# A two-layer transformer and a second block on one core: layer norm behind the experts on VectorE alone, a shift added in TensorE's sums

## The chip, the core and the metric

The kernel runs on one core of a Trainium2 chip. A core has TensorE (matmuls and transposes, results in PSUM), VectorE (DVE), ScalarE (ACT), GpSimd (POOL) and SyncE (SP, which here issues most of the DMAs). Each works off its own queue in order. The metric is the device time of one execution in microseconds, the median of several runs.

## The reference, cut to what matters

A first block (two layers of mixer, layer norm, experts, layer norm) feeds a second block (two layers of three mixers behind a modulated RMS norm). All is f32, 1024 tokens by 1024 features. The places that the change touches are the second layer norm of each layer of the first block, and the input of the second block's first layer:

```python
def layer_norm(x, g, b):
    mu = mean(x); var = mean((x - mu) ** 2)
    return (x - mu) * rsqrt(var + LN_EPS) * g + b

# first block, layers i = 0 and 1
h = layer_norm(ALPHA * h + mix, ln_g[i, 0], ln_b[i, 0])
ffn = hier_moe(h, ...)
h = layer_norm(ALPHA * h + ffn, ln_g[i, 1], ln_b[i, 1])

# second block, layers l = 0 and 1
shift, scale, gate = split(c_act @ ada_w[l] + ada_b[l], 3)
h = rms_norm(x, norm_w[l]) * (1 + scale) + shift
proj = h @ w_in[l]
...
x = x + gate * (mixed @ w_out[l])
```

## The kernel before

The 1024 tokens lie in eight tiles of 128 tokens by 1024 features. Behind each layer of experts a stretch of the program takes these tiles one after the other from the experts' results in DRAM (`yd`) to the matrices that the next gemms read.

`Moe.combine` (L895) loads a tile's two expert rows through SP (L898), adds them on VectorE (L899) and calls `norm_stats`, which takes the statistics (L503, twice 512 columns, then L505 and L507), gets rs as a power on GpSimd (L137, in `Ctx.rsqrt`) and the product -mean x rs on VectorE (L510). `norm_apply` (L514) then scales and moves the tile on ScalarE (L518), multiplies it by the gain on VectorE (L519) and adds the bias on GpSimd (L520).

In the first stretch (L2023 to L2030, behind the first layer's experts) the tile is turned by TensorE at once (`transpose_split`, L98) and split by ScalarE (L80) and VectorE (L81) into two parts for the gemms of `Pooling.run`. Two parts of gemms on the first four tiles run while the last tiles come; from then on the gemms need all eight.

In the second stretch (`feed`, L2070, behind the second layer's experts) the normed tile is stored to `x1d` by SP (L2078). `take_input` squares and sums it on ScalarE (L1201), gets a second power on GpSimd (L1202, L137), multiplies on VectorE by rs and by 1 + scale times the norm's weight (L1209), and adds the shift on GpSimd (L1210). `turn_input` turns the tile in eight transposes of 128 by 128 into PSUM (L1219), ScalarE copies the rounded part out (L80) and VectorE takes the rest (L81). The steps of a tile are spread over the calls of a loop: in step n come the statistics of tile n, the norm of n - 1, the input of n - 2, the turning of n - 3. `first_tiles` (L1264) calls `feed` four times and then has four times 48 matmuls of 256 columns, one group for each two tiles; they write two accumulators, and VectorE's L1278 reads the first of them afterwards. The same `take_input` and `turn_input` serve the second block's second layer, called from `Second.layer`.

`self.mod` holds two rows spread over all 128 partitions (L1184): scale in `mod[:, 0]`, shift in `mod[:, 1]`. `g.one_row` is one row of 128 ones.

The code gives each engine its instructions in program order with waits, but the framework's planner reorders them: it runs the program with its own durations and gives each engine, whenever it is free, the earliest instruction that is ready. What it has put in a queue stays in that order on the chip.

Of the kernel before, what the change touches and what calls it, by code (L numbers as in the profile page):

```python
# [10 lines left out]
F32 = mybir.dt.float32  # L11
# [3 lines left out]
AF = mybir.ActivationFunctionType  # L15
ALU = mybir.AluOpType
# [5 lines left out]
P = 128  # L22
NT = S // P
# [474 lines left out]
def norm_stats(g, pool, z, eps=1e-5):  # L498

    nc = g.nc  # L500
    st = pool.tile([P, 2, 6], F32, tag="ln_st", name=g.name("st"))
    for c in range(2):
        nc.vector.bn_stats(st[:, c], z[:, c * 512:c * 512 + 512])  # L503
    mv = pool.tile([P, 2], F32, tag="ln_mv", name=g.name("mv"))
    nc.vector.bn_aggr(mv, st)  # L505
    v = pool.tile([P, 1], F32, tag="ln_v", name=g.name("v"))
    nc.vector.tensor_scalar(v, mv[:, 1:2], eps, None, op0=ALU.add)  # L507
    rs = g.rsqrt(pool, v, [P, 1])
    sh = pool.tile([P, 1], F32, tag="ln_sh", name=g.name("sh"))
    nc.vector.scalar_tensor_tensor(sh, mv[:, 0:1], -1.0, rs, op0=ALU.mult, op1=ALU.mult)  # L510
    return rs, sh


def norm_apply(g, z, stats, gb):  # L514

    nc = g.nc
    rs, sh = stats
    nc.scalar.activation(z, z, AF.Identity, scale=rs, bias=sh)  # L518
    nc.vector.tensor_mul(z, z, gb[:, 0])  # L519
    nc.gpsimd.tensor_tensor(z, z, gb[:, 1], op=ALU.add)  # L520


def load_gb(g, pool, tag, layer, n):
    gb = pool.tile([P, 2, D], F32, tag=tag, name=g.name("gb"))
    for j, a in enumerate((g.a["ln_g"], g.a["ln_b"])):
        g.nc.sync.dma_start(gb[:, j], a[layer, n:n + 1].broadcast_to([P, D]))
    return gb


class Moe:  # L530
# [4 lines left out]
    @staticmethod  # L535
    def rows(w, kb):
        return w[kb * 512:kb * 512 + 512].rearrange("(a p j) c -> p a (j c)", p=P, j=2), 512
# [357 lines left out]
    def combine(self, t, y, z, pool):  # L895

        g, nc = self.g, self.g.nc
        self.yload = nc.sync.dma_start(y, self.yd.rearrange("(k t p) d -> t p k d", k=2, p=P)[t])  # L898
        nc.vector.tensor_add(z, y[:, 0], y[:, 1])  # L899
        return norm_stats(g, pool, z)  # L900
# [266 lines left out]
class Second:  # L1167
# [34 lines left out]
        nc.vector.tensor_scalar(ss, ss, 1.0 / D, 1e-6, op0=ALU.mult, op1=ALU.add)  # L1202
        return g.rsqrt(pool, ss, [P, 1])

    def take_input(self, t, x, pool, hn=None):
        g, nc = self.g, self.g.nc
        hn = pool.tile([P, D], F32, tag="hn", name=g.name("hn")) if hn is None else hn
        rs = self.rms(x, hn, pool)
        nc.vector.scalar_tensor_tensor(hn, x, rs, self.mod[:, 0], op0=ALU.mult, op1=ALU.mult)  # L1209
        nc.gpsimd.tensor_tensor(hn, hn, self.mod[:, 1], op=ALU.add)  # L1210
        return hn

    def turn_input(self, t, hn, tp=None):
        g, nc = self.g, self.g.nc
        if tp is None:
            tp = self.PS.tile([P, S], F32, tag="tp", name=g.name("tp"))
        tp = tp.rearrange("p (k t) -> p k t", t=P)
        for k in range(KD):
            nc.tensor.transpose(tp[:, k], hn[:, k * P:k * P + P], g.ident)  # L1219
        g.split(tp, *(x[:, :, t % 4 * P:t % 4 * P + P] for x in self.x2[t // 4]))  # L1220


# [719 lines left out]
def program(tc, a, out):  # L1942
    nc = tc.nc
    g = Ctx(tc, a)
# [6 lines left out]
    x1d, x2d = dram("x1d", (S, D)), dram("x2d", (S, D))  # L1951
# [3 lines left out]
    rows = lambda ap, t: ap[t * P:t * P + P]  # L1955

    with pool_of("const") as cp, ExitStack() as r2:
# [40 lines left out]
        with near("rt", 1) as rt:  # L1998
            moe = Moe(g, 0, wp, rt, h, hd, yd)
            gb = load_gb(g, R, "r7", 0, 0)  # L2000
# [14 lines left out]
            gbs = []  # L2015
# [3 lines left out]
        with near("pm", 2) as pool, near("pmps", 4, space=PSUM) as ps:  # L2019
            with near("hT", 1, side="right") as tp:  # L2020
                x2 = [[tp.tile([P, KD, 512], F32R, name=f"pool_{half}{part}") for part in range(2)] for half in range(2)]
                with near("cb0ps", 2, space=PSUM) as tps:
                    h = single(pairs())  # L2023
                    for t in range(NT):
                        if t % 2 == 0:
                            y = H.tile([P, 2, 2, D], F32, tag="wcut", name=g.name("y"))
                        z = h[t]
                        norm_apply(g, z, moe.combine(t, y[:, t % 2], z, pool), gbs[0])
                        sl = slice(t % 4 * P, t % 4 * P + P)
                        g.transpose_split(even_blocks(z.rearrange("p (k d) -> p k d", d=P)), *(x[:, :, sl] for x in x2[t // 4]), tps)  # L2030
                W = []

                def out_piece(pool, tag):
                    W.append(g.split_w(wp.load(proj_piece(a["pool_w_out"][0], len(W))), pool, tag))
                pooling.run(x2, pool, ps, moe.yload.ins, lambda: out_piece(*cut))
            w1 = ExitStack()
            wx = w1.enter_context(near("wo", 2, side="right"))
            out_piece(wx, "w")
            out_piece(wx, "w")
            out_piece(*cut)  # L2040
        wp.use(slots)
        with near("rt1", 1) as rt:
            moe1 = Moe(g, 1, wp, rt, h, hd1, yd1)
            gb = load_gb(g, R, "r7", 1, 0)
# [5 lines left out]
            gbs, L = [], Second(g, H, R, md, zd, mixd, rd, qrd, rrd, x2d)  # L2050
# [14 lines left out]
        with ExitStack() as cb:  # L2065
            pool = cb.enter_context(L.pool("cb1", 3))
            L.start_layer()
            xs, stats, hn = [], [], []

            def feed(q):  # L2070
                for n in range(2 * q + 3 if q else 0, 2 * q + 5):
                    if n < NT:
                        y = R.tile([P, 2, D], F32, tag=f"r{(0, 1, 2, 3, 7)[n % 5]}", name=g.name("y"))
                        xs.append(y[:, 0])
                        stats.append(moe1.combine(n, y, xs[n], pool))
                    if 0 <= n - 1 < NT:
                        norm_apply(g, xs[n - 1], stats[n - 1], gbs[0])
                        nc.sync.dma_start(rows(x1d, n - 1), xs[n - 1])  # L2078
                    if 0 <= n - 2 < NT:
                        hn.append(L.take_input(n - 2, xs[n - 2], pool))  # L2080
                    if n >= 3:
                        L.turn_input(n - 3, hn[n - 3], L.ps("B"))
                if q == 3:
                    cb.close()

            L.layer(feed, x1d, None)
# [31 lines left out]
```

## Time and profile before

| what | us |
|---|---|
| median of three runs | 3568.6 (3566.94 to 3578.99) |
| the profiled execution | 3576.12 |
| its span, first to last instruction | 3574.3 |
| TensorE busy in it | 3308.5 (93%) |
| VectorE busy | 2424.9 (68%) |
| ScalarE busy | 1818.0 (51%) |
| GpSimd busy | 817.6 (23%) |

The profile is one execution. PE is TensorE, PEld its weight loads, DVE VectorE, ACT ScalarE, POOL GpSimd; SPq is SyncE's queue. In a row of the order of time stand the start, the duration, engine, line and operation, what is written and read, how many instructions are merged, and, in brackets, how long the engine was idle before it and what ended that. A row of waits gives the total, how often and the longest. PEclk is TensorE's granted clock as a share of 2.4 GHz; it has two levels, 1.00 and 0.50, and values between are mixtures.

### The profile page before, as it was taken

To read this page: it belongs to the slowest core of one execution; us is meant where nothing else is said; L and a number is where in the kernel's file an instruction comes from. 1 tells how busy PE (TensorE), PEld (TensorE's weight loads), DVE (VectorE), ACT (ScalarE), POOL (GpSimd) and SP (SyncE) were. 2 spreads that over 40 slices of the span, in tenths; PEclk is the share of its full clock that TensorE was granted. 3 is DMA by queue.
4 is the path that set the end of the run, shared out by engine and by line. 5 is a ranking of instruction groups with operands and counts; after the bars stand their busy time and mean duration, and the time that the engine had idled before them with its cause. 6 is when DMAs were issued, how large, how long until landed. Compare 5 with 4: busy or idle time off the path is not lost. (4 is left out here: it accounts for less than half of the span.)

```text
span 3574.3 us, 44065 instructions
## 1 busy us (share of the span) xinstructions
PE 3308.5 (93%) x16808; PEld 2738.9 (77%) x16808; DVE 2424.9 (68%) x2850; ACT 1818.0 (51%) x2505; POOL 817.6 (23%) x583
## 2 busy tenths in 40 slices
PE   8889899899999969989999994899989899998988
PEld 7777787788888858778888883787777788776876
DVE  5564887799999976569999997533366444424653
ACT  3113674388888843337888883122467311243751
POOL 0000441123333322112333324422002113400120
PEclk9999999899999989989999996999999999998999
DMA  6564633499999950259999995210322632122244
GB/s 225 179 209 143 162 85 130 172 359 389 376 379 378 353 214 24 96 177 368 385 390 383 378 348 197 60 30 19 111 77 87 190 111 43 24 80 100 66 136 153
DMA packets 289357, 695.78 MB, mean 195 GB/s; under 512 B 43898, under 2 KB 140956, under 8 KB 272692
## 3 DMA queue, kind: packets, MB, share of 16 engines
q1 hardware_dynamic: 268404, 650.91, 52.4%
q0 software_dynamic: 18432, 33.60, 2.5%
q10 hardware_dynamic: 2304, 8.39, 0.6%
q8 instruction: 135, 2.21, 0.3%
q14 instruction: 82, 0.67, 0.1%
HBM read 625.59 MB, written 98.66 MB: 203 GB/s over the span
## 5 line engine op out<-in xcount | busy, mean ns | idle before, releaser
L81 DVE TENSOR_TENSOR wcut<-wraw,wcut 128x2048 fp32r<-128x2048 f32 (+1 forms) x401 | 902.6, 2268 | 74.9 <-ACT wcut L80 74.8
L80 ACT ACTIVATE wcut<-wraw 128x2048 fp32r<-128x2048 f32 (+1 forms) x401 | 753.9, 1900 | 132.0 <-PE accy L87 98.0
L85 PE MATMUL gu<-wcut,xgh 128*128 128x512 f32 x1024 | 410.2, 401 | 0.0
L87 PE MATMUL gu<-wcut,xgl 128*128 128x512 f32 x1024 | 404.6, 395 | 0.0
L86 PE MATMUL gu<-wcut,xgh 128*128 128x512 f32 x1024 | 402.7, 393 | 0.0
L806 POOL DMA_INDIRECT yd<-yo,idx x64 | 173.5, 2711 | 794.5 <-DVE yo L805 788.0
L85 PE MATMUL A<-h,whi 128*128 128x512 f32 (+1 forms) x736 | 286.6, 390 | 6.2 <-ACT h L80 3.3
L87 PE MATMUL A<-h,wlo 128*128 128x512 f32 (+1 forms) x736 | 281.5, 383 | 3.8 <-DVE wlo L81 3.8
L86 PE MATMUL A<-h,whi 128*128 128x512 f32 (+1 forms) x736 | 282.1, 383 | 1.0 <-DVE h L81 1.0
L80 ACT ACTIVATE whi<-wraw 128x1024 fp32r<-128x1024 f32 (+2 forms) x86 | 71.1, 855 | 333.4 <-PE A L86 248.1
L85 PEld LDWEIGHTS gu<-wcut,xgh 128*128 128x128 f32 x1024 | 194.7, 190 | 38.3 <-ACT xgh L80 0.5
L86 PEld LDWEIGHTS gu<-wcut,xgh 128*128 128x128 f32 x1024 | 193.6, 189 | 39.5
L87 PEld LDWEIGHTS gu<-wcut,xgl 128*128 128x128 f32 x1024 | 193.1, 189 | 39.5 <-DVE xgl L81 0.5
L81 DVE TENSOR_TENSOR wlo<-wraw,whi 128x1024 fp32r<-128x1024 f32 (+2 forms) x86 | 82.5, 975 | 176.6 <-ACT whi L80 176.2
L87 PE MATMUL accy<-wcut,hl 128*128 128x512 f32 x512 | 201.9, 394 | 0.3 <-DVE hl L81 0.3
L86 PE MATMUL accy<-wcut,hh 128*128 128x512 f32 x512 | 200.6, 392 | 0.0
L85 PE MATMUL accy<-wcut,hh 128*128 128x512 f32 x512 | 199.0, 389 | 1.6 <-ACT hh L80 1.6
L746 POOL DMA_INDIRECT xg<-hd,idx x64 | 184.8, 2888 | 56.6 <-DVE idx L736 37.7
L85 PEld LDWEIGHTS A<-h,whi 128*128 128x128 f32 x736 | 144.5, 197 | 34.1 <-ACT h L80 4.4
L87 PEld LDWEIGHTS A<-h,wlo 128*128 128x128 f32 x736 | 143.8, 195 | 31.3 <-DVE wlo L81 4.7
L86 PEld LDWEIGHTS A<-h,whi 128*128 128x128 f32 x736 | 144.6, 196 | 27.5 <-issue 3.1
L1703 POOL TENSOR_TENSOR z<-z,lo 128x1024 f32<-128x1024 f32 x8 | 19.0, 2376 | 476.6 <-DVE r L81 177.4
(508 smaller groups left out, 7825.1 us busy)
## 6 DMA issues: line engine op xcount, KB each, us to landing
wraw<-in_moe_w_gate SPq DMA_DIRECT2D x128, 1024.0 KB
wraw<-in_moe_w_up SPq DMA_DIRECT2D x128, 1024.0 KB
wraw<-in_moe_w_down SPq DMA_DIRECT2D x128, 1024.0 KB
spare<-in_ada_w SPq DMA_DIRECT2D x48, 512.0 KB
wraw<-in_w_in SPq DMA_DIRECT2D x40, 512.0 KB
y<-yd SPq DMA_DIRECT2D x16, 1024.0 KB
wraw<-in_attn_w_qkv SPq DMA_DIRECT2D x12, 1024.0 KB
mx<-mixd SPq DMA_DIRECT2D x24, 512.0 KB
```

What stands on the lines that cost most here:

```text
L80: self.nc.scalar.activation(hi, src, AF.Copy)
L81: (lo_eng or self.nc.vector).tensor_tensor(lo, src, hi.bitcast(F32), op=ALU.subtract)
L85: mm(out, wh, xh, start=start, stop=False)
L86: mm(out, wh, xl, start=False, stop=False)
L87: mm(out, wl, xh, start=False, stop=stop)
L746: self.g.nc.gpsimd.indirect_dma_start(out=xg, out_offset=None, in_=self.hd, in_offset=bass.IndirectOffsetOnAxis(ap=idx, axis=0), bounds_ch ...
L806: st = nc.gpsimd.indirect_dma_start(out=self.yd, out_offset=bass.IndirectOffsetOnAxis(ap=yidx, axis=0), in_=y, in_offset=None, bounds_chec ...
L1703: nc.gpsimd.tensor_tensor(z, z, rb, op=ALU.mult)
```

## The change

`norm_stats` gives back the mean and rs and no longer forms -mean x rs. `norm_apply` becomes two operations of VectorE, (z - mean) x gain and then that x rs + bias; ScalarE and GpSimd have no part in it. This holds for both stretches. In `feed`, `take_input` leaves out GpSimd's add of the shift, and `turn_input` puts behind each transpose a matmul that adds, into the same sum in PSUM, the shift's 128 features times a row of ones. The order of the loop's steps is changed: in step n come the statistics of tile n, the turning of n - 2, the input of n - 1, the norm of n and its store. The second block's second layer calls both functions with their old behaviour.

```diff
 (norm_stats)
-    rs = g.rsqrt(pool, v, [P, 1])
-    sh = pool.tile([P, 1], F32, tag="ln_sh", name=g.name("sh"))
-    nc.vector.scalar_tensor_tensor(sh, mv[:, 0:1], -1.0, rs, op0=ALU.mult, op1=ALU.mult)
-    return rs, sh
+    return mv[:, 0:1], g.rsqrt(pool, v, [P, 1])

 def norm_apply(g, z, stats, gb):
-    nc = g.nc
-    rs, sh = stats
-    nc.scalar.activation(z, z, AF.Identity, scale=rs, bias=sh)
-    nc.vector.tensor_mul(z, z, gb[:, 0])
-    nc.gpsimd.tensor_tensor(z, z, gb[:, 1], op=ALU.add)
+    mean, rs = stats
+    g.nc.vector.scalar_tensor_tensor(z, z, mean, gb[:, 0], op0=ALU.subtract, op1=ALU.mult)
+    g.nc.vector.scalar_tensor_tensor(z, z, rs, gb[:, 1], op0=ALU.mult, op1=ALU.add)

-    def take_input(self, t, x, pool, hn=None):
+    def take_input(self, t, x, pool, hn=None, shift=True):
...
-        nc.gpsimd.tensor_tensor(hn, hn, self.mod[:, 1], op=ALU.add)
+        if shift:
+            nc.gpsimd.tensor_tensor(hn, hn, self.mod[:, 1], op=ALU.add)

-    def turn_input(self, t, hn, tp=None):
+    def turn_input(self, t, hn, tp=None, shift=False):
...
             nc.tensor.transpose(tp[:, k], hn[:, k * P:k * P + P], g.ident)
+            if shift:
+                nc.tensor.matmul(tp[:, k], self.mod[0:1, 1, k * P:k * P + P], g.one_row, start=False, stop=True, skip_group_check=True)

 (feed)
-                for n in range(2 * q + 3 if q else 0, 2 * q + 5):
+                for n in range(2 * q + 2 if q else 0, 2 * q + 4):
                     if n < NT:
...
                         stats.append(moe1.combine(n, y, xs[n], pool))
+                    if n >= 2:
+                        L.turn_input(n - 2, hn[n - 2], L.ps("B"), shift=True)
                     if 0 <= n - 1 < NT:
-                        norm_apply(g, xs[n - 1], stats[n - 1], gbs[0])
-                        nc.sync.dma_start(rows(x1d, n - 1), xs[n - 1])
-                    if 0 <= n - 2 < NT:
-                        hn.append(L.take_input(n - 2, xs[n - 2], pool))
-                    if n >= 3:
-                        L.turn_input(n - 3, hn[n - 3], L.ps("B"))
+                        hn.append(L.take_input(n - 1, xs[n - 1], pool, shift=False))
+                    if n < NT:
+                        norm_apply(g, xs[n], stats[n], gbs[0])
+                        nc.sync.dma_start(rows(x1d, n), xs[n])
```

## Rows read from the trace of the kernel before

**Rows 1.** The page's forty slices of the span: TensorE busy and its clock, tenths.
```profile
PE   8889899899999969989999994899989899998988
...
PEclk9999999899999989989999996999999999998999
```

**Rows 2.** Waits in the second stretch, 2165 to 2270: total us, times, longest.
```profile
PE B L1219 <- POOL hn L1210: 52.6, 7, 33.7
```

**Rows 3.** Waits in the first stretch, 1284 to 1360.
```profile
PE tp L98 <- POOL h L520: 33.0, 7, 19.7
```

**Rows 4.** Order of time, one tile's period in the second stretch.
```profile
2222.86 1.28 DVE L1209 SCALAR_TENSOR_TENSOR hn<-y,rs_y,mod 128x1024 f32<-128x1024 f32 x1 [0.36 <-POOL rs_y L137]
...
2224.06 1.28 DVE L503 BATCH_NORM_STATS2 st<-y 128x6 f32<-128x512 f32 x2
2224.29 2.34 POOL L1210 TENSOR_TENSOR hn<-hn,mod 128x1024 f32<-128x1024 f32 x1 [1.46 <-DVE hn L1209]
...
2225.26 2.45 DVE L519 TENSOR_TENSOR y<-y,gb 128x1024 f32<-128x1024 f32 x1
...
2227.77 1.21 DVE L899 TENSOR_TENSOR y<-y 128x1024 f32<-128x1024 f32 x1
2227.79 3.41 POOL L520 TENSOR_TENSOR y<-y,gb 128x1024 f32<-128x1024 f32 x1 [1.16 <-DVE y L519]
...
2228.97 1.21 DVE L81 TENSOR_TENSOR h<-B,h 128x1024 fp32r<-128x1024 f32 x1
...
2232.26 1.29 DVE L1209 SCALAR_TENSOR_TENSOR hn<-y,rs_y,mod 128x1024 f32<-128x1024 f32 x1 [0.36 <-POOL rs_y L137]
```

**Rows 5.** Order of time, second stretch: first add, two turnings, first use of an accumulator.
```profile
2178.31 1.23 DVE L899 TENSOR_TENSOR y<-y 128x1024 f32<-128x1024 f32 x1 [9.56 <-DMA y<-yd]
...
2251.83 1.97 PE L1219 MATMUL B<-ident,hn 128*128 128x128 f32 x8 [2.51 <-POOL hn L1210]
2256.85 1.03 PE L1219 MATMUL B<-ident,hn 128*128 128x128 f32 x8
...
2263.91 1.23 DVE L1278 TENSOR_TENSOR ta<-A,r 128x1024 f32<-128x1024 f32 x1 [3.71 <-PE A L87]
```

**Rows 6.** Order of time, first stretch: first add and last split.
```profile
1292.97 1.23 DVE L899 TENSOR_TENSOR h<-y 128x1024 f32<-128x1024 f32 x1 [9.31 <-DMA y<-yd]
...
1350.80 1.37 DVE L81 TENSOR_TENSOR pool<-tp,pool 128x512 fp32r<-128x512 f32 x2 [2.43 <-ACT pool L80]
```

**Rows 7.** Windows: length, busy us of PE, PEld, DVE, ACT, POOL; PEclk, DMA share, GB/s.
```profile
1353.00:1383.00 30.00, 30.00 (x130) 24.14 (x129) 23.30 (x26) 7.04 (x9) 11.23 (x11) 1.00 0.11 36
...
2375.00:2382.00 7.00, 7.00 (x21) 5.55 (x21) 1.22 (x1) 5.59 (x5) 0.00 (x0) 0.51 0.44 75
```

**Rows 8.** Lines: durations (min/median/max ns); last row: idle time before L494.
```profile
L491 DVE SCALAR_TENSOR_TENSOR h<-h,mv,gb x16: 1271/1275/1281, 579.3 to 1562.9; 128x1024 f32<-128x1024 f32 x16
...
L137 POOL TENSOR_TENSOR rs_y<-v,mhalf x32: 539/1444/1887, 579.5 to 2239.6; 128x1 f32<-128x1 f32 x32
...
  POOL rs_y L137: 4.8, 12
```

**Rows 9.** Order of time on TensorE, small matmuls with 16 rows and with one.
```profile
2372.25 0.38 PE L1386 MATMUL B<-gb,ones_f 1*128 1x128 f32 x2
2372.48 0.38 PE L1385 MATMUL B<-gw,r 16*128 16x128 f32 x2
...
2375.26 0.63 PE L1385 MATMUL B<-gw,r 16*128 16x128 f32 x2
2375.69 0.63 PE L1386 MATMUL B<-gb,ones_f 1*128 1x128 f32 x2
```

**Rows 10.** Window with the second stretch's last gemms of 256 columns, columns as rows 7.
```profile
2259.00:2263.00 4.00, 4.00 (x36) 4.00 (x35) 1.21 (x1) 0.00 (x0) 0.00 (x0) 1.00 0.00 0
```

**Rows 11.** Window over most of the second stretch, columns as rows 7.
```profile
2208.00:2258.00 50.00, 32.89 (x177) 29.98 (x178) 34.77 (x44) 16.40 (x21) 35.15 (x21) 0.69 0.35 119
```

**Rows 12.** Order of time on SP's queue: the first four loads, and the last.
```profile
2173.02 2.60 SPq L898 DMA_DIRECT2D y<-yd  x4
...
2214.83 0.36 SPq L898 DMA_DIRECT2D y<-yd  x1
```

## What the change will do to the time

> **What bounds the kernel now.** I first read the page in forty slices [rows 1]: TensorE is nearly full everywhere, except in the slices that begin at 1251 us and 2144 us (digits 6 and 4), where its granted clock falls too. Both follow a layer of experts, and both hold the code that the diff touches: tile by tile, `combine`, `norm_apply` and the turning of the tile by TensorE. Then I read who waits for whom. In the second block's start TensorE waits 52.6 us in seven waits for GpSimd's add of the shift (L1210) [rows 2]; behind the first experts it waits 33.0 us for GpSimd's add of the norm (L520) [rows 3]. So TensorE is starved by a chain of VectorE and GpSimd.
>
> The order of time shows how one tile of the second stretch costs 9.40 us, from one multiplication by rs (L1209) at 2222.86 to the next at 2232.26 [rows 4]. L1209 ends at 2224.14; GpSimd's shift follows, 2224.29 to 2226.63. VectorE's L519 starts at 2225.26 but needs 2.45 us, where L899, the same operation on the same shape, needs 1.21: it gets on only when the shift is done. L899 follows at 2227.77, and L520, issued at 2227.79, needs 3.41 us where GpSimd's other add of the same shape took 2.34: now GpSimd waits for VectorE. Then come two small powers, and L1209 is next. An add of GpSimd and an operation of VectorE with two inputs in SBUF take turns here, while L503 (one input) ran beside the shift at its 1.28. The chain of five such operations and the powers is the 9.4 us.
>
> The second stretch runs from the first add at 2178.31 to 2263.91, where VectorE gets the first accumulator [rows 5]: 85.6 us. The first stretch runs from 1292.97 to the last split of tile 7, ending at 1350.80 + 1.37 = 1352.17 [rows 6]: 59.2 us. TensorE works with hardly a gap behind each (30.00 of 30 us in 1353 to 1383 [rows 7]; the slices behind the second stand at 8 and 9 [rows 1]), so that a microsecond won at an end is won for the kernel.
>
> **The norm without ScalarE and GpSimd.** Per tile and stretch go the pass of ScalarE, L510, L519 and L520; two scalar_tensor_tensor of VectorE come. L491, the same operation on the same shape with a mean from the same kind of tile, takes 1.275 us [rows 8]. Start to start it is 1.20: L503 starts 1.20 us behind L1209, a third operation of this form [rows 4]. The Trainium skill, page Vector Engine (DVE) Microarchitecture Reference, section Points that are easy to get wrong, says that this operation halves its throughput when both sources lie in SBUF and are not bf16; by that rule each would cost about 2.4 us, and the time would be that of the fourth rival below. The row speaks against it.
>
> VectorE's sum per tile in the second stretch, start to start: add 1.13, statistics 1.20 (each row less the 0.08 by which neighbours overlap), three small ones 0.3, two new ones 2.40, L1209 1.20, split 1.20 (L81; two halves in the first stretch): 7.4 us. In the first stretch L1209 and one small one are missing: 6.1 us. What hid VectorE's extra 1.2 us per tile was the wait for GpSimd; that is gone, so VectorE is the nearest bound. One wait stays: the power (L137) on GpSimd. It is 0.54 us alone, but its median in the layer norms, where the same two operations stand around it, is 1.444, and L494 waited for it 12 times for 4.8 us, 0.4 each [rows 8]. One such power in the first stretch, two in the second: periods of 6.5 and 8.2 us. The other end is no wait at all: 6.1 and 7.4.
>
> **The shift in TensorE's sums.** Eight adds of GpSimd (2.34 each) go; each of 64 transposes gets a matmul of one row by 128 columns in f32. The nearest row is L1386, the same shape: two passes, the next pair 0.23 us later at the 2.4 GHz level and 0.43 at 1.2 GHz [rows 9]. A tile's eight transposes took 1.03 us at the upper level and 1.97 at the lower [rows 5], start to start 0.11 and 0.22 each. So turning a tile costs 8 x 0.34 = 2.7 us or 8 x 0.65 = 5.2 us, 1.8 or 3.4 more than the transposes alone. Its gemms are 24 matmuls per tile, 0.12 us apart at the upper level [rows 10], half the speed below: 2.9 or 5.1. TensorE thus needs 5.6 to 10.3 us per tile; at the mean clock of this stretch now, 0.69 [rows 11], 5.6/0.69 = 8.1. That is level with VectorE's 8.2. The longer turning also lengthens a wait: L81 waits for ScalarE's copy (1.1) and that for the turning, and behind L81 on VectorE stand the next L1209 and norm. From L1209's end, the norm's last step (1.6) and the next add and statistics (2.6) give cover for 4.2 us; the turning and the copy need 3.8 at the upper level, 6.3 at the lower, where VectorE would stand 2.1. I add 0.4 to 8.2 and take 8.6 as the period; the ends are 7.4 and 10.3.
>
> **The steps nearer together.** A tile's norm now follows in the step of its statistics, its turning two steps behind, where it was three. At the end two steps run out instead of three. The store to x1d moves with the norm to the same step, on SP's queue ahead of the next y load that has no buffer yet. What it holds back has room: the last y load was issued at 2214.83 and used at 2227.77, 13 us later [rows 4, 12], against 5.3 us from the first issue, 2173.02, to its use [rows 5, 12]. I cost it at nothing; without that cover a late load would cost up to those 5.3 us once. On GpSimd nothing long stands ahead of a power any more.
>
> **The sum.** Second stretch, from the first add: first tile to the end of its norm 5.9 (1.2 + 1.3 + 0.4 + 2.6 + 0.4), second 6.8 (no split yet), six at 8.6, is 64.3; the last tile's square, power and L1209 3.6, its turning at mean clock 3.9, ScalarE's half 1.1, and 48 matmuls 7.2 (between 5.8 at the upper level and 8.4 at 0.69): 80.1 us against 85.6, **5.5 us won**. First stretch: 5.9 + 7 x 6.5 = 51.4, turning and two halves of splitting 3.3: 54.7 against 59.2, 4.5. Of that I take 1.0 back: TensorE will have done the first half's gemms some 10 us early, and is likelier to be at 1.2 GHz when tile 7 comes. The only nearby price is 7.00 us of busy time at 0.51 behind a fall [rows 7], some 3.5 lost; none lost is the other end. **3.5 us won.** Together 9.0. The profiled execution took 3576.1 us (span 3574.3 and 1.8 around it), 7.5 above the median of the three runs; nothing suggests that the stretches are what made it longer, so I subtract from the median: 3568.6 - 9.0 = **3559.6**. The page's other stages keep their operations; layer 2 of the second block still adds its shift on GpSimd.
>
> **Rivals.** First, the clock rises: with the starving gone, TensorE keeps 2.4 GHz and VectorE alone bounds. Second stretch 12.7 + 6 x 8.2 + 3.6 + 2.7 + 1.1 + 5.8 = 75.1, 10.5 won; first 4.5: **3553.6**, and with no wait for powers 3544.5 (16.4 and 7.7). For it: TensorE has less idle time. Against it: clock 0.69 now, and much of the new work is one row high.
>
> Second, on the other side: TensorE's clock becomes the bound. In the midst of L1385 and L1386, small matmuls like the new ones, the distance of the pairs goes from 0.23 to 0.43 [rows 9], and TensorE, busy all the time, stays at 0.51 for 7 us [rows 7]. If the new ones do that to every tile, the decisive point is a mean clock of 0.65 (5.6/0.65 = 8.6, my period). At 0.6, 9.5 us per tile: 12.7 + 57 + 3.6 + 4.5 + 1.1 + 9.6 = 88.5, 2.9 lost, 2 won in the first: **3569.5**. At 1.2 GHz throughout, 12 until the first turning, then 8 x 5.2 + 192 x 0.21 + 1.1, is 95.0: 9.4 lost, 2 won, 3576.
>
> Third, the change doesn't do what it says: the chain with GpSimd stays, through the powers. If VectorE's two-input operations stand back to back, each power waits out one (1.444) before its user starts: periods of 7.4 + 3.0 = 10.4 and 6.1 + 1.5 = 7.6. Then 12.7 + 62.4 + 3.6 + 3.9 + 1.1 + 7.2 = 90.9 and 62.4: 5.3 and 3.2 lost, **3577**. For it: that median. Against it: only 0.4 of it reached L494.
>
> Fourth, the new operations cost twice the row, 2.4 us each: 19.2 more in each stretch makes 99.3 and 73.9, 13.7 and 14.7 lost: **3597**. L491's 16 executions, none above 1.281, speak against it.
>
> **How the numbers follow.** Forecast 47%, clock rises 24%, clock bounds 20%, powers 7%, twice the row 2%. The forecast's own range is 3553 to 3566. The range reaches from 3546, most of the first rival, to 3573, past the middle of the second; the rest, some 2 in 10, is left out. What a measurement can tell from no change is about 0.3%, 10.7 us: below 3557.9 lies a third of the forecast (16%) and nearly all of the first rival (22%), so faster 38%; above 3579.3 the tails of the last three, 6%; within, 56%.
>
> **What would show it.** Right: no GpSimd operation above 1.5 us in either stretch but the gather; VectorE's tile period 8.2 to 9 us in the second; its end within 78 to 82 us of the first add; 54 to 57 us in the first. Wrong: a mean clock under 0.65 or above 0.9 in the second stretch; TensorE's turning not ended when ScalarE wants it, tile after tile; L137 ahead of each L1209 with a wait near 1.4; the new operations longer than 1.3 us; a y load that VectorE waits for; or a gain at the first end that the pooling's gemms give back to a lower clock.

## The result and the profile after

The change made the kernel slower: 3598.1 us (median of four runs, 3597.0 to 3599.3) against 3567.8 (four runs, 3565.2 to 3579.0). The ratio is estimated at 1.0074 (95% interval 1.0062 to 1.0086); the two medians by themselves would give 1.0085. The prediction was 3559.6, with a range of 3546 to 3573. The profiled executions differ by less, 3594.8 against 3574.3 us of span, since that of before lay above its median; the 20.5 us between them are the ones that the traces can place.

The ends of the two stretches in the kernel after, in order of time (start, duration, engine, line, operation, what it waited for); they answer [rows 5] and [rows 6]:

```profile
1294.03 1.23 DVE L894 TENSOR_TENSOR h<-y 128x1024 f32<-128x1024 f32 x1 [9.15 <-DMA y<-yd]
...
1347.33 0.69 DVE L81 TENSOR_TENSOR pool<-tp,pool 128x512 fp32r<-128x512 f32 x1 [0.16 <-ACT pool L80]
...
2173.92 1.23 DVE L894 TENSOR_TENSOR y<-y 128x1024 f32<-128x1024 f32 x1 [10.44 <-DMA y<-yd]
...
2287.31 1.23 DVE L1277 TENSOR_TENSOR ta<-A,r 128x1024 f32<-128x1024 f32 x1 [6.51 <-PE A L87]
```

The first stretch runs from 1294.03 to 1347.33 + 0.69 = 1348.02: 54.0 us where before took 59.2. The second runs from 2173.92 to 2287.31: 113.4 us where before took 85.6. The whole difference is the sum of five pieces: the first stretch starts 1.1 later, is 5.2 shorter, 0.2 shorter is what lies between the stretches, the second is 27.8 longer, and 2.9 shorter is what follows it: 20.5. So the norm's half of the change worked, and everything was lost in the second stretch.

Who waits for whom there (total us, times, longest); of [rows 2] nothing is left, GpSimd's add being gone:

```profile
ACT h L80 <- PE B L1218: 61.4, 8, 12.7
...
DVE h L81 <- ACT h L80: 41.1, 8, 9.8
...
PE B L1216 <- DVE hn L1204: 26.2, 1, 26.2
```

TensorE waits 26.2 us for its first tile, and after that only 4.2 us in five short waits. VectorE's split (L81) now waits for ScalarE's copy eight times, once for each tile, and ScalarE for the last matmul of the shift (L1218). The bound has changed its engine. TensorE's groups in that stretch (operation, shapes, count; busy us, mean ns; idle before them):

```profile
L1218 PE MATMUL B<-ones_f,mod 1*128 1x128 f32 x128 | 44.8, 445 | 0.0
L1216 PE MATMUL B<-ident,hn 128*128 128x128 f32 x64 | 27.1, 423 | 26.2 <-DVE hn L1204 26.2
```

The two overlap; together, turning takes 63.5 us of the 113. Two pieces of it in order of time, the first at TensorE's lower level (1.2 GHz), the second at its upper (2.4 GHz); they answer [rows 9] and the turnings of [rows 5]:

```profile
2187.01 0.48 PE L1216 MATMUL B<-ident,hn 128*128 128x128 f32 x1 [26.18 <-DVE hn L1204]
2187.42 0.79 PE L1218 MATMUL B<-ones_f,mod 1*128 1x128 f32 x2
2188.14 0.47 PE L1216 MATMUL B<-ident,hn 128*128 128x128 f32 x1
2188.55 0.79 PE L1218 MATMUL B<-ones_f,mod 1*128 1x128 f32 x2
...
2225.60 0.33 PE L1216 MATMUL B<-ident,hn 128*128 128x128 f32 x1
2225.86 0.48 PE L1218 MATMUL B<-ones_f,mod 1*128 1x128 f32 x2
2226.27 0.33 PE L1216 MATMUL B<-ident,hn 128*128 128x128 f32 x1
```

A transpose and its matmul take 1.13 us at the lower level (2187.01 to 2188.14) and 0.67 at the upper (2225.60 to 2226.27), so that a tile's eight take 9.0 or 5.4 us. The prediction had 5.2 or 2.7. By windows (length, busy us of PE, PEld, DVE, ACT, POOL, then the granted clock, DMA share, GB/s), the stretch as a whole and its pieces, to be held against [rows 11]:

```profile
2173.92:2287.31 113.39, 96.03 (x362) 70.16 (x363) 59.88 (x80) 17.27 (x25) 14.20 (x16) 0.59 0.32 113
2187.00:2206.00 19.00, 18.10 (x48) 10.86 (x48) 11.08 (x17) 4.17 (x6) 3.02 (x4) 0.50 0.70 222
2206.00:2232.00 26.00, 24.20 (x97) 18.01 (x97) 14.88 (x21) 4.41 (x7) 3.05 (x4) 0.63 0.23 81
2232.00:2258.00 26.00, 24.42 (x97) 18.41 (x97) 15.74 (x21) 4.23 (x6) 4.02 (x4) 0.63 0.22 81
2258.00:2287.31 29.31, 29.31 (x122) 22.89 (x123) 6.15 (x6) 3.31 (x5) 0.54 (x1) 0.61 0.05 19
```

TensorE is busy from the first turning on, at 0.50 to 0.63 of its clock, and VectorE for some 60% of each piece or less. Page slices after, which answer [rows 1]: the slice that begins at 1258 us is a 6 as before; the one at 2157 us is a 6 where before had a 4, and its clock a 5 where before had a 6.

```profile
PE   8889899899999969989999996999989899998988
...
PEclk9999999899999989989999995899999999998999
```

So TensorE is fuller in the slice of the loss: it first stands idle until the experts have ended and the first tile has come, and is then full but slow.

### The profile page after: what moved, and what is told of

The parts are those of the page before. It is cut to its first block, busy times and chain, and to the rows that moved or that the text cites. A ratio compares the mean times of both kernels' runs of the same rounds, so it can differ in the third digit from the quotient of the medians.

```text
span 3594.8 us, 44282 instructions
## 1 busy us (share of the span) xinstructions
PE 3358.7 (93%) x16936; PEld 2766.6 (77%) x16936; DVE 2424.5 (67%) x2850; ACT 1797.1 (50%) x2489; POOL 762.8 (21%) x559
## 5 line engine op out<-in xcount | busy, mean ns | idle before, releaser
L81 DVE TENSOR_TENSOR wcut<-wraw,wcut 128x2048 fp32r<-128x2048 f32 (+1 forms) x401 | 902.7, 2268 | 73.7 <-ACT wcut L80 73.6
L85 PE MATMUL gu<-wcut,xgh 128*128 128x512 f32 x1024 | 410.2, 401 | 0.0
L87 PE MATMUL gu<-wcut,xgl 128*128 128x512 f32 x1024 | 404.8, 395 | 0.0
L86 PE MATMUL gu<-wcut,xgh 128*128 128x512 f32 x1024 | 402.8, 393 | 0.0
L85 PE MATMUL A<-h,whi 128*128 128x512 f32 (+1 forms) x736 | 288.8, 393 | 6.2 <-ACT h L80 3.3
L87 PE MATMUL A<-h,wlo 128*128 128x512 f32 (+1 forms) x736 | 284.3, 386 | 3.9 <-DVE wlo L81 3.9
L86 PE MATMUL A<-h,whi 128*128 128x512 f32 (+1 forms) x736 | 284.6, 387 | 0.9 <-DVE h L81 0.9
L85 PEld LDWEIGHTS gu<-wcut,xgh 128*128 128x128 f32 x1024 | 194.8, 190 | 38.3 <-ACT xgh L80 0.5
L86 PEld LDWEIGHTS gu<-wcut,xgh 128*128 128x128 f32 x1024 | 193.6, 189 | 39.6
L87 PEld LDWEIGHTS gu<-wcut,xgl 128*128 128x128 f32 x1024 | 193.1, 189 | 39.4 <-DVE xgl L81 0.5
L87 PE MATMUL accy<-wcut,hl 128*128 128x512 f32 x512 | 201.9, 394 | 0.3 <-DVE hl L81 0.3
L81 DVE TENSOR_TENSOR wlo<-wraw,whi 128x1024 fp32r<-128x1024 f32 (+2 forms) x86 | 82.5, 975 | 177.3 <-ACT whi L80 176.9
L86 PE MATMUL accy<-wcut,hh 128*128 128x512 f32 x512 | 200.7, 392 | 0.0
L85 PE MATMUL accy<-wcut,hh 128*128 128x512 f32 x512 | 199.0, 389 | 1.6 <-ACT hh L80 1.6
L85 PEld LDWEIGHTS A<-h,whi 128*128 128x128 f32 x736 | 146.8, 200 | 34.1 <-ACT h L80 4.1
L87 PEld LDWEIGHTS A<-h,wlo 128*128 128x128 f32 x736 | 146.2, 199 | 31.9 <-DVE wlo L81 4.7
L86 PEld LDWEIGHTS A<-h,whi 128*128 128x128 f32 x736 | 146.9, 200 | 27.8 <-issue 3.3
L85 PE MATMUL acc<-r,mx 128*128 128x512 f32 x256 | 104.1, 407 | 16.9 <-DMA mx<-mixd 16.9
```

Of the source, the lines that this page charges most:

```text
L81: (lo_eng or self.nc.vector).tensor_tensor(lo, src, hi.bitcast(F32), op=ALU.subtract)
L85: mm(out, wh, xh, start=start, stop=False)
L86: mm(out, wh, xl, start=False, stop=False)
L87: mm(out, wl, xh, start=False, stop=stop)
```

## The experiments

The theory after reading the trace: TensorE loses time each time it goes from a transpose to a one-row matmul and back, and so becomes the bound of the second stretch. Its rivals: the one-row matmuls cost that much wherever they stand; the matmul waits because it adds to what the transpose ahead is still writing; the loss is not the shift's at all but the order's or the norm's. Each ratio below is against runs of the kernel before on the same chip. All stretches together, measured as above, each in the one profiled execution of its kernel; the clock is the granted one from the second stretch's window:

| kernel | first, us | second, us | clock in second | ratio to before (95%) |
|---|---|---|---|---|
| before | 59.2 | 85.6 | 0.65 | 1 |
| after | 54.0 | 113.4 | 0.59 | 1.0074 (1.0062 to 1.0086) |
| e1 shift by GpSimd | 54.0 | 84.9 | 0.64 | 0.9985 (0.9976 to 0.9995) |
| e2 no shift | 54.7 | 75.7 | 0.65 | 0.9960 (0.9946 to 0.9974) |
| e3 matmuls behind all transposes | 54.0 | 83.8 | 0.67 | 0.9981 (0.9972 to 0.9991) |
| e4 matmul one block behind | 54.0 | 104.0 | 0.63 | 1.0043 (1.0028 to 1.0057) |
| e5 before, shift alone | 59.2 | 108.6 | 0.61 | 1.0061 (1.0046 to 1.0076) |
| e6 before, norm alone | 55.0 | 81.1 | 0.66 | 0.9974 (0.9964 to 0.9984) |
| e8 four rows, 512 columns | 54.0 | 77.1 | 0.68 | 0.9951 (0.9935 to 0.9968) |
| e9 128 rows, alternating | 54.0 | 74.4 | 0.83 | 0.9965 (0.9951 to 0.9980) |
| e10 before, order alone | 59.0 | 89.0 | 0.67 | 1.0005 (0.9995 to 1.0014) |
| e11 as e9, old order | 54.6 | 76.3 | 0.79 | 0.9968 (0.9959 to 0.9978) |
| e12 e9 again | 54.7 | 74.4 | 0.83 | 0.9966 (0.9953 to 0.9979) |

### Is it the shift? e1, e2 and e5

e1 gives the shift back to GpSimd and keeps the rest:

```diff
-  L.turn_input(n - 2, hn[n - 2], L.ps("B"), shift=True)
+  L.turn_input(n - 2, hn[n - 2], L.ps("B"))
-  hn.append(L.take_input(n - 1, xs[n - 1], pool, shift=False))
+  hn.append(L.take_input(n - 1, xs[n - 1], pool))
```

> The changed kernel with one part undone: GpSimd adds the shift again, and the 64 one-row matmuls are gone; VectorE's layer norm and the nearer steps stay. If those matmuls are what lost 27.8 us in the second stretch (113.4 us where before took 85.6), TensorE's turning falls back to about 1 to 2 us per tile and the bound is VectorE with GpSimd: five two-input operations of VectorE (add, two of the norm, L1204, split: 5.9 us) plus a shift of 2.3 that takes turns with some of them, 8.2 to 9.4 us per tile, a stretch of 75 to 86 us and a time of 3560 to 3571. If something else lost them (the order of the steps, the norm on VectorE), the stretch stays above 105 us and the time above 3590.

Measured: 3568.0 us against 3573.0, second stretch 84.9. The 28 us are the shift's. But the stretch only comes back to where before had it.

e2 changes the first of the two lines alone, so that nobody adds the shift:

```diff
-  L.turn_input(n - 2, hn[n - 2], L.ps("B"), shift=True)
+  L.turn_input(n - 2, hn[n - 2], L.ps("B"))
```

> The changed kernel without the second block's first shift at all: nobody adds it (the output lacks it from the second block on). It gives the floor for any way of adding it. With VectorE alone as bound at 7.4 to 8.2 us per tile I expect a second stretch of 70 to 78 us and 3555 to 3563; if TensorE's low clock or the order of the steps were the bound without the matmuls too, the stretch stays above 90 us and the time above 3575.

Measured: 3559.1, second stretch 75.7, both as expected. In order of time, what VectorE still waits for there:

```profile
2209.23 1.28 DVE L1204 SCALAR_TENSOR_TENSOR hn<-y,rs_y,mod 128x1024 f32<-128x1024 f32 x1 [0.95 <-POOL rs_y L137]
...
2213.69 1.22 DVE L81 TENSOR_TENSOR h<-B,h 128x1024 fp32r<-128x1024 f32 x1 [0.79 <-ACT h L80]
```

A power of GpSimd costs it 0.95 in such a tile, and ScalarE's copy 0.79: the floor is VectorE's, with small waits.

e5 is the kernel before with the shift alone moved:

```diff
...
   nc.tensor.transpose(tp[:, k], hn[:, k * P:k * P + P], g.ident)
+  if shift:
+      nc.tensor.matmul(tp[:, k], self.mod[0:1, 1, k * P:k * P + P], g.one_row, start=False, stop=True, skip_group_check=True)
...
```

> The kernel before with the shift alone moved: 64 one-row matmuls alternating with the transposes, as in the changed kernel; old norm, old order. If TensorE's change of height is the loss by itself, a turning takes 9.0 us at 1.2 GHz and 5.4 at 2.4, the second stretch becomes 105 to 118 us and the time 1.006 to 1.010 of before's (about 20 to 33 us more), with no need of the other two parts. If the loss needs the nearer steps (a turning two steps behind leaves less room), the stretch stays under 100 and the time under 1.004.

Measured: 3591.8 against 3571.5, second stretch 108.6, with the old norm and the old order. Its pairs, in order of time, have the same length as in the kernel after, 1.13 us:

```profile
2197.30 0.47 PE L1220 MATMUL B<-ident,hn 128*128 128x128 f32 x1
2197.71 0.79 PE L1222 MATMUL B<-ones_f,mod 1*128 1x128 f32 x2
2198.43 0.47 PE L1220 MATMUL B<-ident,hn 128*128 128x128 f32 x1
```

The loss needs neither of the other two parts.

### What in the shift? e3, e4 and e9

e3 runs the same 16 instructions per tile, sorted:

```diff
   for k in range(KD):
       nc.tensor.transpose(tp[:, k], hn[:, k * P:k * P + P], g.ident)
-      if shift:
-          nc.tensor.matmul(tp[:, k], ..., start=False, stop=True, skip_group_check=True)
+  for k in range(KD if shift else 0):
+      nc.tensor.matmul(tp[:, k], ..., start=False, stop=True, skip_group_check=True)
```

This kernel and e4 do not compute the reference: each transpose marks a start of its own, as in the change, but other transposes now come before the matmul that is to add to it, and the sums no longer hold (e8, with a start only at the first block of each half, has them right). The instructions and their sizes are the same as in the change.

> The changed kernel with the same 8 transposes and 8 one-row matmuls per tile, but all transposes first and then all matmuls, so that neither alternates with the other. Theory A, that alternating costs the time (each instruction waits until the one ahead has left the array): a turning falls to 8 x 0.34 = 2.7 us at 2.4 GHz and 8 x 0.65 = 5.2 at 1.2 GHz, as priced from the rows of L1386, where it measured 5.4 and 9.0; the second stretch is 80 to 97 us and the time 3565 to 3582. Theory B, that a one-row matmul with its own weights costs 0.46 and 0.72 us wherever it stands: turning 5.4 and 9.0 again, stretch above 108, time 3593 to 3603.

Measured: 3565.9 against 3573.0. Two turnings in order of time, one at each level:

```profile
2185.34 1.97 PE L1216 MATMUL B<-ident,hn 128*128 128x128 f32 x8 [26.19 <-DVE hn L1204]
2187.24 3.78 PE L1218 MATMUL B<-ones_f,mod 1*128 1x128 f32 x16
...
2212.35 1.03 PE L1216 MATMUL B<-ident,hn 128*128 128x128 f32 x8
2213.31 2.05 PE L1218 MATMUL B<-ones_f,mod 1*128 1x128 f32 x16
```

A turning takes 1.90 + 3.78 = 5.7 us at the lower level and 0.96 + 2.05 = 3.0 at the upper, near the prediction's 5.2 and 2.7. So it is not the one-row matmuls as such: the alternation costs 9.0 - 5.7 = 3.3 us a tile at 1.2 GHz and 5.4 - 3.0 = 2.4 at 2.4 GHz. It has 16 changes of kind per tile (the last one to the gemms) where e3 has 2; over the 14 more, that is 0.24 and 0.17 us each.

e4 keeps the alternation, but the matmul adds to the block before the last one:

```diff
-  for k in range(KD):
-      nc.tensor.transpose(tp[:, k], ...)
-      if shift:
-          nc.tensor.matmul(tp[:, k], ...)
+  for k in range(KD + 1):
+      if k < KD:
+          nc.tensor.transpose(tp[:, k], ...)
+      if shift and k:
+          j = k - 1
+          nc.tensor.matmul(tp[:, j], ...)
```

> The changed kernel, still alternating, but the shift's matmul stands one block behind: transpose k+1 lies between transpose k and the matmul that adds to its block. Of theory A this tells two forms apart. If the matmul waits because it adds to what the transpose just ahead of it is still writing, the lag takes the wait away: a turning of 2.7 to 3.5 us at 2.4 GHz and 5.2 to 6.5 at 1.2 GHz, time 3565 to 3585. If TensorE drains whenever a transpose and a matmul follow each other, whatever they write, the pair stays at 0.67 and 1.13 us and the time at 3593 to 3603. Theory B expects the latter too.

```profile
2185.05 0.79 PE L1220 MATMUL B<-ones_f,mod 1*128 1x128 f32 x2
2185.77 0.47 PE L1217 MATMUL B<-ident,hn 128*128 128x128 f32 x1
2186.18 0.79 PE L1220 MATMUL B<-ones_f,mod 1*128 1x128 f32 x2
```

The pairs keep their 1.13 us (2185.05 to 2186.18) although the matmul no longer touches what the instruction ahead of it wrote. The time, 3589.5 against 3573.0, fell short of the expected 3593 to 3603: at both ends of a tile two instructions of a kind now stand together, which saves two changes of sixteen, some 0.4 us a tile, and the granted clock was 0.63 where the kernel after had 0.59. That the sum waits for its own block is refuted.

e9 leaves the alternation and the sum as the change has them, and gives the matmul all 128 rows (the shift stands in every row of its tile; the other operand is ones in row 0 and zeros below):

```diff
-  nc.tensor.matmul(tp[:, k], self.mod[0:1, 1, k * P:k * P + P], g.one_row, ...)
+  nc.tensor.matmul(tp[:, k], self.mod[:, 1, k * P:k * P + P], self.first_row, ...)
...
```

> The changed kernel, still alternating and each matmul adding to the block just transposed, but the shift's matmul takes all 128 rows: the weights are the shift's 128 equal rows, the other operand is ones in row 0 and zeros below, so that the sum is the same. Batched, a transpose and a one-row matmul took 0.24 + 0.47 us at 1.2 GHz and 0.12 + 0.26 at 2.4; alternating they took 1.13 and 0.67, whether or not the matmul adds to the block just written. Theory A1: TensorE drains because the height changes between 128 rows and 1. Then the pair falls to about 0.71 and 0.38 us, a turning to 5.6 and 3.0, the second stretch to 80 to 88 us (batched: 83.8) and the time to 0.996 to 1.000 of before's. Theory A2: it drains because a transpose and a true matmul follow each other, whatever their height. Then the pair stays at 1.13 and 0.67, the stretch above 105 and the time above 1.005 of before's.

```profile
2184.41 0.42 PE L1216 MATMUL B<-ident,hn 128*128 128x128 f32 x1
2184.62 0.64 PE L1218 MATMUL B<-first_row,mod 128*128 128x128 f32 x2
2185.05 0.42 PE L1216 MATMUL B<-ident,hn 128*128 128x128 f32 x1
...
2191.25 0.27 PE L1216 MATMUL B<-ident,hn 128*128 128x128 f32 x1
2191.36 0.39 PE L1218 MATMUL B<-first_row,mod 128*128 128x128 f32 x2
2191.58 0.27 PE L1216 MATMUL B<-ident,hn 128*128 128x128 f32 x1
...
2245.03 1.23 DVE L1277 TENSOR_TENSOR ta<-A,r 128x1024 f32<-128x1024 f32 x1 [3.70 <-PE A L87]
```

Measured: 3561.2 against 3573.6, second stretch 74.4. The pair is 0.64 us at the lower level and 0.33 at the upper, alternating all the same, a little less than A1's 0.71 and 0.38; the stretch is shorter than its 80 to 88, at a higher clock (last section). With 128 times as many rows a pair takes about half the time, and the difference, (1.13 - 0.64)/2 = 0.24 and (0.67 - 0.33)/2 = 0.17 us for each change, is about what e3 gave. This settles it: TensorE pays for each change between operands of 128 rows and of one, not for transpose and matmul following each other. The Trainium skill, page TensorEngine Tiling (Array Packing), section Tiling Modes, says that changing the tiling mode, and not just the tile, drains TensorE. It gives no price and does not say that a one-row matmul is in a mode of its own; if it is, the traces agree, and the price is the 0.24 and 0.17 us. Read so, that rule spoke against this change; I did not weigh it.

### The other two parts alone: e6 and e10

e6 is the kernel before with the two new operations of the norm (the first half of the change's diff), e10 the kernel before with the new order of `feed` (its last part).

> The kernel before with the new layer norm alone (two operations of VectorE); old order of steps, GpSimd adds the shift. The first stretch, which has only this change, falls from 59.2 to 54 us as in the changed kernel. In the second, five two-input operations of VectorE take turns with one of GpSimd: if the norm is what moves the chain, 80 to 83 us and 0.997 to 0.998 of before's; if the nearer order is needed for it, 84 to 87 and 0.998 to 1.000.

> The kernel before with the new order of the steps alone: a tile's norm in the step of its statistics, its turning two steps behind. ScalarE, VectorE and GpSimd do the norm as before and GpSimd adds the shift. The prediction cost the order at nothing but the one step less at the end. If that holds, the chain of VectorE and GpSimd keeps its 9.4 us and the second stretch is 82 to 87 us, time 0.998 to 1.002 of before's. If the norm in the step of its statistics makes VectorE wait for the chain of ScalarE and GpSimd within a step, the period grows above 10.5 us and the stretch above 92, time above 1.002.

Measured: the norm alone 3563.7 against 3573.6, with 55.0 and 81.1 us, as the first of its cases had it; the order alone 3576.9, with 59.0 and 89.0. The order, while GpSimd adds the shift, makes the second stretch 3.4 us longer: the time is one expected of an order that costs nothing, the stretch lies above the 82 to 87 of that case and short of the other's 92. With the new norm it is 84.9 - 81.1 = 3.8 (e1 against e6). What it puts side by side shows in the durations of the add in `combine` (min/median/max ns), e6 first, then e1:

```profile
L894 DVE TENSOR_TENSOR y<-y x8: 1170/1210/1225, 2176.2 to 2225.0; 128x1024 f32<-128x1024 f32 x8
```

```profile
L894 DVE TENSOR_TENSOR y<-y x8: 1164/1718/2797, 2172.6 to 2224.7; 128x1024 f32<-128x1024 f32 x8
```

In the new order the next tile's add runs beside GpSimd's shift and takes turns with it, as L519 did in [rows 4]. By windows over the stretch VectorE is busy for 68.5 us in e1 and 65.8 in e6, 2.7 of the 3.8; the rest I have not traced.

### Versions that beat both: e8, e11 and e12

e8 turns all eight blocks first, marking a start only at the first of each half so that the sums hold, and adds the shift of four blocks at once:

```diff
...
-  nc.tensor.transpose(tp[:, k], hn[:, k * P:k * P + P], g.ident)
...
+  nc.tensor.matmul(tp[:, k], hn[:, k * P:k * P + P], g.ident, is_transpose=True, start=not shift or k % 4 == 0, stop=True, skip_group_check=shift)
+  for half in range(2 if shift else 0):
+      for part in self.rows4:
+          nc.tensor.matmul(tp[:, 4 * half:4 * half + 4], part[:, half], self.pick, start=False, stop=True, skip_group_check=True)
```

> A version meant to beat both kernels: the eight transposes first (only the first of each half marked as a start, so that the sums hold), then the shift for four blocks at once: four matmuls of 4 rows by 512 columns in fp32r (high and low part of the shift, two halves; the weights are four rows of the shift, the other operand picks the row of the block). TensorE changes its height twice per tile and not sixteen times, and a matmul of 512 columns takes 0.21 or 0.42 us by the gemms: a turning of 1.0 + 0.9 = 1.9 us at 2.4 GHz and 1.9 + 1.7 = 3.6 at 1.2 GHz, against 1.0 and 1.9 without a shift. If the turning's length is all that parts the batched kernel (83.8 us) from the one without a shift (75.7), the second stretch is 77 to 81 us and the time 0.9955 to 0.998 of before's. If the clock of TensorE falls with short matmuls of few rows, it is no better than batched: 83 us and above, 0.998 or more.

```profile
2185.77 1.97 PE L1225 MATMUL B<-ident,hn 128*128 128x128 f32 x8 [26.06 <-DMA y<-yd]
2187.67 0.79 PE L1228 MATMUL B<-pick,rows_h 4*128 4x512 f32 x1
2188.26 0.62 PE L1228 MATMUL B<-pick,rows_l 4*128 4x512 f32 x1
2188.69 0.62 PE L1228 MATMUL B<-pick,rows_h 4*128 4x512 f32 x1
```

Measured: 3558.9 against 3573.6; the second stretch, 77.1, is as expected, the ratio just below what was expected. The first wide matmul is followed 0.59 us later, the next 0.43: 0.16 us of a change of height shows there. Nearly as much shows ahead of it: the eight transposes take 1.90 us up to the first wide matmul, as in e3, where 8 x 0.22 is 1.76. So a change is some 0.3 us at the lower level here, but there are two of them per tile instead of sixteen.

e11 is e9 with the old `feed`, e12 is e9 once more.

> VectorE's norm and the shift as 128-row matmuls between the transposes (the second stretch took 74.4 us so), but in the old order of the steps. The order alone made the second stretch 89.0 where before took 85.6, and with the new norm and GpSimd's shift 84.9 where the old order took 81.1. If that price belongs to the order as such, this falls to 70 to 72 us and 0.9955 of before's or below; if it comes from what the order puts side by side on VectorE and GpSimd (without GpSimd's adds there is nothing left to collide with), the old order costs its one step more at the end: 74 to 80 us, 0.996 to 0.998.

> The kernel of the 128-row matmuls once more, beside the one in the old order, for the interval: 0.9955 to 0.9975 of before's by the earlier run's 0.9965. If its low first time came from one stretch's clock, the median lies at 0.997; if the full height keeps TensorE at 2.4 GHz in the second stretch (0.83 there, where one-row matmuls gave 0.59 to 0.68), the granted clock of that stretch is 0.78 to 0.88 again and the stretch 73 to 77 us.

Measured: 3561.7 and 3559.4 against 3571.5; second stretches 76.3 and 74.4. Without GpSimd's adds the nearer steps win 1.9 us instead of losing 3.4, so the order's price was what it put side by side, as the second of e11's two answers has it. The repeat gave the same stretch and clock as e9. e8, e9 and e11 all beat both kernels. Their intervals don't part them, and what follows the second stretch, the same code in all, took from 1299.8 to 1312.6 us among the profiled runs of all kernels. e6 beats both too, with the norm alone and the shift still on GpSimd, and its interval overlaps these; only the second stretch (81.1 us against 74.4 to 77.1) shows what moving the shift adds.

## Why the prediction was wrong, step by step

**The step that failed** is the price of the turning: "The nearest row is L1386, the same shape". The shape was the same, the neighbours were not. In [rows 9] one-row matmuls alternate with ones of 16 rows, and no row of mine had a one-row operand beside a 128-row one. The term was 5.2 or 2.7 us per tile; it measured 9.0 or 5.4. The bounds I kept for it were two clock levels of one row, not two kinds of neighbour.

The trace of before had the price next to those very rows. These are the two ends of the run that [rows 9] is cut from, where matmuls of 128 rows (L85 to L87) stand beside it:

```profile
2371.61 0.39 PE L87 MATMUL A<-h,wlo 128*128 128x512 f32 x1
2371.93 0.48 PE L1385 MATMUL B<-gw,r 16*128 16x128 f32 x2
...
2376.25 0.80 PE L85 MATMUL A<-h,whi 128*128 128x512 f32 x1
2376.84 0.63 PE L86 MATMUL A<-h,whi 128*128 128x512 f32 x1
```

Going in, at the upper level, L1385 comes 0.32 us behind L87 and L1386 (2372.25) 0.32 behind that, where 0.23 and 0.22 are the distances before and after: 0.19 us for the change from 128 rows to 16. Coming out, at the lower level, L85 follows L1386 (2375.69) after 0.56 and L86 follows L85 after 0.59, where 0.43 is the distance on both sides: 0.29 us for the change from one row to 128. Times sixteen a tile, that is 3.0 or 4.6 us on top of 2.7 or 5.2, an estimate from these rows of 5.7 or 9.8 us where 5.4 or 9.0 was measured.

**What that did to the bound.** TensorE needed 5.6 to 10.3 us per tile in the prediction, level with VectorE at the clock of the time; it came to 25.6 and 26.0 us for two tiles (L81 at 2206.21, 2231.85 and 2257.85), 12.9 each. Put into the sum: 12.7 + 6 x 12.9 + 3.6 + 9.0 + 1.1 + 8.4 = 112.2, where 113.4 was measured; that they lie so near is in part luck, since the last tiles came some 11 us apart and VectorE's 3.6 was no longer in the way. By TensorE itself the 113.4 are 13.1 us until its first turning, 63.5 of turning, 32.6 of other matmuls and 4.3 of gaps, rounded. The mechanism was the second rival's, TensorE as bound, and its sign on the second stretch. Its cause was not: at its own 0.6 of the clock (0.59 measured) and the row's price it gave 88.5 (87.5, if 5.6/0.6 is taken as 9.3 and not 9.5), and the other 25 us are the changes of height: 128 of them at 0.17 to 0.24 are 22 to 31. Of the signs of being wrong that the prediction lists, the first two came: a mean clock under 0.65, and a turning not ended when ScalarE wants it, for all eight tiles. The fourth rival's 3597, so near the 3598.1, is chance: it had 73.9 and 99.3 us for stretches that took 54.0 and 113.4.

**With the right price the period holds, the ends do not.** e3 is nearly the change as the prediction saw it. VectorE's adds there stand at 2187.00 and, four tiles on, at 2221.89: 8.7 us per tile, forecast 8.6. Its second stretch was 83.8 where I had 80.1, its time 0.9981 of before's where I had 0.9975. But two larger misses partly cancel in it: from the last tile's add to the accumulator are 34.2 us, and my sum has 8.6 + 3.6 + 3.9 + 1.1 + 7.2 = 24.4 there, while the first tiles are quicker than its 5.9, 6.8 and 8.6 (14.8 from the first add to the fourth, not 21.3). When the last tile is added, the tile ahead of it still has its norm to come too (L514 at 2225.90 and 2231.73), and four tiles have their split to come.

**The norm** was right. Three lines of L514 and L515, durations as min/median/max ns, which answer [rows 8]:

```profile
L514 DVE SCALAR_TENSOR_TENSOR h<-h,mv,gb x8: 1276/1292/1300, 1296.9 to 1341.6; 128x1024 f32<-128x1024 f32 x8
...
L515 DVE SCALAR_TENSOR_TENSOR h<-h,rs_y,gb x8: 1282/1288/1301, 1299.2 to 1343.3; 128x1024 f32<-128x1024 f32 x8
L515 DVE SCALAR_TENSOR_TENSOR y<-y,rs_y,gb x8: 1268/1277/1280, 2179.1 to 2259.0; 128x1024 f32<-128x1024 f32 x8
```

They take the 1.275 us of L491, none of the 32 above 1.301, so the fourth rival is refuted here too. The rule of the Trainium skill, page Vector Engine (DVE) Microarchitecture Reference, section Points that are easy to get wrong, from which that rival took its 2.4 us, is not borne out for this operation and shape. The first stretch took 54.0 (forecast 54.7).

**What the clock takes back** did not show. I had 1.0 of the first stretch's gain go to a lower clock behind it. Between the stretches the kernel after took 825.9 us, before 826.1, so all of the 5.2 arrived; the other kernels lie between 825.4 and 827.7 there, with the old norm (e5 826.5, e10 827.7) as with the new. That spread is wider than the 1.0, but it does not lean against the new norm.

**The order** was put at nothing, but for the one step less at the end, which is in the sum. Beside a shift on TensorE it won 1.9 us (e11 against e9 and e12), so it is not what failed. While GpSimd adds the shift it costs 3.4 and 3.8, and nothing in the prediction would have told that: my cover was argued for the store and the y loads, and those did hold (VectorE waits for no y load but the first); the add that comes to stand beside GpSimd's was not looked at.

**The third rival** (powers) was not it, but its wait is in every fast version: up to 0.96 us ahead of L1204 (L1213 in e8), where I had 0.4.

**The first rival** (the clock rises) was not the change's outcome, but e9, with 128 rows, comes near it: clock 0.83, a tile's turning at 8 x 0.33 = 2.6, a second stretch of 74.4 where it had 75.1.

## What to carry to other kernels

Price a small matmul by a row with the same neighbours, not only the same shape, and read the rows at both ends of a run of small matmuls, where the neighbours change: between operands of 128 rows, one of a single row cost TensorE two changes of 0.17 to 0.24 us here, about what the matmul itself takes. Give it all rows (zeros do), or sort it behind the others, before thinking of another engine. And a step that is moved is to be held against what the engines that take turns with it do at its new place, not only against queues and buffers.

## What the runs showed that was not expected

TensorE's granted clock in the second stretch was higher in the kernels whose small matmuls have all 128 rows. The whole stretch in e3 (one row, sorted) and in e9 (128 rows, alternating), windows with columns as above:

```profile
2172.24:2256.04 83.80, 63.35 (x362) 59.29 (x363) 59.69 (x81) 17.29 (x25) 14.20 (x16) 0.67 0.43 154
```

```profile
2170.61:2245.03 74.42, 49.63 (x362) 47.71 (x363) 59.60 (x80) 17.17 (x25) 14.20 (x16) 0.83 0.49 174
```

The two run the same number of instructions on TensorE. With full rows the clock was 0.83 (0.83 again in e12, 0.79 in e11); with one row or four it was 0.59 to 0.68, and without any shift 0.65. So 64 added matmuls made the stretch no longer than without the shift, 74.4 against e2's 75.7. What parts the clocks is not shown: from run to run the time for which TensorE is busy changes with the rows (63.4 us in e3, 49.6 in e9, 40.4 in e2), and nothing was tried that changes one alone. A TensorE that was busy for 18.1 of 19 us stood at 0.50 all that time in the kernel after (window 2187 to 2206).
